# Seven products of quarters in the feed-forward, and attention's value products in one row

## The chip, the cores and the metric

One core of one Trainium2 chip runs the whole program. The metric is the device time of one execution in microseconds. Five engines work beside each other: TensorE (PE, matmul), VectorE (DVE), ScalarE (ACT), GpSimd (POOL) and the queue that starts transfers (SP). Each takes its own instructions in order and waits on the others through semaphores.

## What is computed

One step of a two-layer network for 1024 latent and 256 context tokens of width 1024. Each layer mixes by attention, a recurrence and a long convolution, projects the result out, and ends in a gated feed-forward of inner width 2816:

```python
    mix = jnp.concatenate([att, lru, hy], axis=-1)
    x = x + g1 * (mix @ lp['w_out'])
    h2 = rmsnorm(x, lp['norm2_w']) * (1 + sc2) + sh2
    x = x + g2 * ((jax.nn.silu(h2 @ lp['ffn_w1']) * (h2 @ lp['ffn_w3'])) @ lp['ffn_w2'])
```

## The kernel before, in words

Tokens lie along the free axis and channels along the partitions. The tokens come in three blocks: l0 and l1 (512 latent tokens each) and cc (256 context tokens). All projections are computed at nearly fp32 accuracy: each operand is cut into a high part (rounded to fp32r by ScalarE, L142) and a low part (the difference, on VectorE or GpSimd, L143), and `mm3` (L134) issues three matmuls, high by high, high by low, low by high (L136 to L138). One k-tile of 128 channels by one m-tile of 128 outputs is thus three matmuls of 512 columns for a latent block.

`w_out` (L431) computes the output projection in groups of m-tiles, adds it to the tokens x (L458) and sums squares (`ss_add`, L341). After the last m-tile of a block comes `norm`: TensorE sums the squares over channels (`nps`, L362), VectorE makes the reciprocal root in a dozen tiny steps (L149 to L158), TensorE spreads it (L369), and per k-tile VectorE multiplies (L376), ScalarE adds the shift and rounds (L378) and VectorE or GpSimd makes the low part (L379, L143). These two parts, h, feed the next products.

`ffn` (L470) runs over 22 chunks of 128 inner channels. Per chunk it loads three weight tiles of 512 KB (w1, w3, w2), cut by ScalarE and GpSimd, and per block computes `up` (8 k-tiles of w1 into `pu` and 8 of w3 into `pv`, the context both into `puv`; then the gate on ScalarE and VectorE, L491 to L493, and the cut of g on VectorE) and `down` (8 m-tiles of w2 by g into `py`, each added to x at once, L506). The order of a chunk is up l0, up cc, up l1, down l0, down cc, down l1. In the last chunk the norm of the next layer (or, in the last layer, the store) of each block stands behind its last `down`.

Attention of the latents has 32 units: 4 pairs of heads, 4 runs of 256 queries, layers 0 and 1. A unit does for two heads: scores (`sps`, L685), their evacuation with a running minimum (VectorE, L686), the exponential (ScalarE, L688), transposes of the weights (`tps`, L701) with copies to SBUF by VectorE (L703) or ScalarE (L705), then in `attn_out` the products with the values (`pvo`, L718: 10 tiles of keys by two heads), and four products of 64 rows that spread the reciprocal sums over the head's channels (L722), a product on the result (L727) and its store. A scheduler places all instructions by due times worked out from their order in the program, and pools of buffers with a fixed number each set when a buffer may be written again: weights as loaded (`wst`, 3), weights cut (`whl`, 4).

Of the kernel before, what the change touches and what calls it, by code (L numbers as in the profile page):

```python
# [20 lines left out]
DEPTH = 2  # L21
# [12 lines left out]
FT = 3  # L34
WG = (1, 2)
QT, PQ, PK = 3, 5, 3
# [7 lines left out]
KTB, CMB = 1, 1  # L44
KPIECES = (4, 6, 0, 2)
KORDER = (4, 5, 6, 7, 0, 1, 2, 3)
PE, QX = 4, 2
MORDER = (6, 8, 4, 7, 9, 0, 5, 1, 10, 2, 11, 3, 12, 13, 14, 15)

# [22 lines left out]
class Net:  # L72
# [11 lines left out]
    def setup(self):  # L84
# [13 lines left out]
        for s, n, t in ((self.lat, "l", LAT), (self.ctxs, "c", SEQ)):  # L98
# [12 lines left out]
            s.fe = [self.dp.tile([2, t // 128, 128, 512], F32, name=f"fe_{n}{l}") for l in range(DEPTH)]  # L111
            s.mix = [self.dp.tile([D, t], F32, name=f"mix_{n}{l}") for l in range(DEPTH)]
# [240 lines left out]
    def norm(self, s, l, j, bi, hp, tp):  # L353
# [4 lines left out]
        tag = "s" if l == j == 0 and bi else "n"  # L358
# [9 lines left out]
        for t in range(nt):  # L368
            nc.tensor.matmul(p2[:, t * 128:(t + 1) * 128], r[:, 2 * t:2 * t + 1].to_broadcast([128, 128]),  # L369
                             self.ident, start=True, stop=True)  # L370
        self.h_new(s, bi, hp)
# [59 lines left out]
    def w_out(self, l, hp, tp, xp):  # L431
# [3 lines left out]
        for s, bi, b0, N in blks:  # L435
# [12 lines left out]
            if s.lat:  # L448
                self.x_new(s, bi, xp, 2)
                for d in range(0, 8, XD):  # L450
                    nc.sync.dma_start(s.x[bi][:, d:d + XD], s.xd[bi][:, d:d + XD])

        def one(m, w, s, bi, b0, N):
# [3 lines left out]
            xs = s.x[bi][:, m]  # L457
            nc.vector.scalar_tensor_tensor(xs, ps, self.mod(l, s, 2, m), xs, ALU.mult, ALU.add)  # L458
            self.ss_add(s, tp, s.ss[bi], xs, m)

        for g in GROUPS:
            ws = [self.wtile(self.a["w_out"][l][:, m * 128:(m + 1) * 128].rearrange("(k p) m -> p k m", p=128))
                  for m in g]
            for b in blks:
                for m, w in zip(g, ws):
                    one(m, w, *b)
                if g[-1] == 7:
                    self.norm(b[0], l, 1, b[1], hp, tp)

    def ffn(self, l, hp, pool, last, mods):  # L470
        nc, a = self.nc, self.a
        for c in range(NFF):
            cs = slice(c * 128, (c + 1) * 128)
            w1 = self.wtile(a["ffn_w1"][l][:, cs].rearrange("(k p) m -> p k m", p=128))
            w3 = self.wtile(a["ffn_w3"][l][:, cs].rearrange("(k p) m -> p k m", p=128))
            w2 = self.wtile(a["ffn_w2"][l][cs, :].rearrange("p (k m) -> p k m", m=128))
            gs = {}

            def up(s, bi, b0, N):
                gb = pool.tile([128, 2, N], F32R, tag="g" + s.n, name="g", bufs=3 if s.lat else 1)  # L480
                gs[s, bi] = gb
                if s.lat:
                    pu, pv = self.ps(s, "pu"), self.ps(s, "pv")
                else:
                    pb = self.ps(s, "puv", (128, 2, 256))
                    pu, pv = pb[:, 0], pb[:, 1]
                for w, p in ((w1, pu), (w3, pv)):
                    for k in range(8):
                        self.mm3(p, w[:, 0, k], w[:, 1, k], *self.hk(s, bi, k), k == 0, k == 7)
                t = pool.tile([128, N], F32, tag="ft", name="ft", bufs=FT)  # L490
                nc.scalar.activation(t, pu, AF.Tanh, scale=0.5)  # L491
                nc.vector.scalar_tensor_tensor(t, t, 1.0, pu, ALU.add, ALU.mult)  # L492
                nc.vector.scalar_tensor_tensor(t, t, 0.5, pv, ALU.mult, ALU.mult)  # L493
                self.split(t, gb[:, 0], gb[:, 1], nc.vector)

            def down(s, bi, b0, N):
                gb = gs[s, bi]
                per = 512 // N
                for d0 in range(0, 8, per):
                    ps = self.ps(s, "py", (128, per, N))  # L500
                    for dd in range(per):
# [860 lines left out]
```

## Time and profile before

| | us |
|---|---|
| three runs | 3825.55, 3826.84, 3830.46 (median 3826.84) |
| profiled execution, whole time | 3824.65 |
| its span | 3822.9 |
| busy: TensorE | 3676.4 |
| VectorE | 2148.4 |
| ScalarE | 1155.5 |
| GpSimd | 786.5 |

Busy times overlap; the share of TensorE in the span says that it is nearly always at work. Durations printed for matmuls overlap too, so their pace is read from the distance between starts.

### The profile page before, as it was taken

The numbers are of one execution on the slowest core, as the hardware profiler recorded it, in microseconds if no ns is written. First come the engines' busy times: TensorE is split into PE (matmuls) and PEld (weight loads), VectorE is DVE, ScalarE is ACT, GpSimd is POOL, SyncE is SP. The second block draws the span as 40 slices with busy tenths as digits, with TensorE's granted clock in tenths as the row PEclk, the third lists the DMA queues.
The fourth block names the chain that finished last, engine by engine and source line by source line (L and its number), as shares of the span: only waits on it lengthen the run. The fifth ranks groups of instructions, "written<-read, shape, count | busy, mean of one in ns | idle before, by whom it ended". The sixth has DMA issues, their size and how long they took to land. (4 is left out here: it accounts for less than half of the span.)

```text
span 3822.9 us, 50093 instructions
## 1 busy us (share of the span) xinstructions
PE 3676.4 (96%) x19866; PEld 2936.9 (77%) x19866; DVE 2148.4 (56%) x4242; ACT 1155.5 (30%) x1903; POOL 786.5 (21%) x488
## 2 busy tenths in 40 slices
PE   6999988999999999999998999999999999999999
PEld 3667766676788888888886787666688888888887
DVE  6554567786364544454455674776636444544554
ACT  4333433654231111111124543455423111111111
POOL 3332133100231111211123332200133112111110
PEclk7999999999999999999998999999999999999999
DMA  7554764211211111111113344520311111111111
GB/s 267 176 196 163 231 222 147 69 48 57 87 34 36 43 39 34 39 39 39 34 57 95 110 160 151 181 71 26 108 45 39 39 34 41 38 39 34 45 34 55
DMA packets 292016, 324.90 MB, mean 85 GB/s; under 512 B 26286, under 2 KB 213728, under 8 KB 288454
## 3 DMA queue, kind: packets, MB, share of 16 engines
q1 hardware_dynamic: 288646, 307.02, 24.7%
q0 software_dynamic: 3136, 14.68, 1.2%
q8 instruction: 156, 2.56, 0.3%
q14 instruction: 78, 0.64, 0.1%
HBM read 244.51 MB, written 77.14 MB: 84 GB/s over the span
## 5 line engine op out<-in xcount | busy, mean ns | idle before, releaser
L143 POOL TENSOR_TENSOR whl<-wst,whl 128x1024 fp32r<-128x1024 f32 x177 | 428.6, 2423 | 1976.8 <-ACT whl L142 1921.2
L506 DVE SCALAR_TENSOR_TENSOR x_l<-py,modc,x_l 128x512 f32<-128x512 f32 x704 | 486.2, 738 | 5.1 <-PE py L138 4.8
L142 ACT ACTIVATE whl<-wst 128x1024 fp32r<-128x1024 f32 x180 | 190.1, 1057 | 805.8 <-issue 710.5
L137 PE MATMUL py<-g,whl 128*128 128x512 f32 (+1 forms) x1056 | 376.3, 356 | 0.0
L136 PE MATMUL py<-g,whl 128*128 128x512 f32 (+1 forms) x1056 | 371.4, 358 | 1.5 <-ACT g L142 1.5
L138 PE MATMUL py<-g,whl 128*128 128x512 f32 (+1 forms) x1056 | 369.3, 356 | 0.0
L136 PE MATMUL wps<-h,whl 128*128 128x512 f32 (+1 forms) x768 | 285.0, 373 | 5.6 <-ACT h L378 2.8
L137 PE MATMUL wps<-h,whl 128*128 128x512 f32 (+1 forms) x768 | 283.6, 370 | 2.8 <-POOL h L143 2.0
L492 DVE SCALAR_TENSOR_TENSOR ft<-ft,pu 128x512 f32<-128x512 f32 x88 | 60.6, 689 | 399.7 <-ACT ft L491 399.4
L138 PE MATMUL wps<-h,whl 128*128 128x512 f32 (+1 forms) x768 | 282.9, 369 | 0.0
L136 PE MATMUL pu<-h,whl 128*128 128x512 f32 x704 | 278.5, 396 | 3.2 <-ACT h L378 3.2
L137 PE MATMUL pu<-h,whl 128*128 128x512 f32 x704 | 278.1, 395 | 1.6 <-DVE h L379 1.0
L138 PE MATMUL pv<-h,whl 128*128 128x512 f32 x704 | 278.3, 395 | 0.0
L137 PE MATMUL pv<-h,whl 128*128 128x512 f32 x704 | 277.7, 395 | 0.0
L136 PE MATMUL pv<-h,whl 128*128 128x512 f32 x704 | 277.7, 394 | 0.0
L138 PE MATMUL pu<-h,whl 128*128 128x512 f32 x704 | 277.5, 394 | 0.0
L493 DVE SCALAR_TENSOR_TENSOR ft<-ft,pv 128x512 f32<-128x512 f32 x88 | 60.5, 687 | 345.0 <-PE pv L138 344.7
L138 PEld LDWEIGHTS py<-g,whl 128*128 128x128 f32 x1056 | 198.9, 188 | 32.7
L136 PEld LDWEIGHTS py<-g,whl 128*128 128x128 f32 x1056 | 198.7, 189 | 30.2 <-ACT g L142 1.9
L688 ACT ACTIVATE pq<-pq,mn 128x1280 f32<-128x1280 f32 (+1 forms) x160 | 190.3, 1190 | 104.5 <-DVE pq L686 100.1
L137 PEld LDWEIGHTS py<-g,whl 128*128 128x128 f32 x1056 | 199.6, 189 | 27.0
L701 PE MATMUL tps<-ident,pq 128*128 128x128 f32 x1344 | 202.3, 278 | 14.3 <-ACT pk L705 8.0
(310 smaller groups left out, 7961.6 us busy)
## 6 DMA issues: line engine op xcount, KB each, us to landing
wst<-in_ffn_w_dram SPq DMA_DIRECT2D x132, 512.0 KB
wst<-in_w_mod_dram SPq DMA_DIRECT2D x68, 512.0 KB
wst<-in_w_in_dram SPq DMA_DIRECT2D x32, 512.0 KB
wst<-in_w_mod_dram SPq DMA_DIRECT2D x14, 1024.0 KB
pT_l<-pe SPq DMA_DIRECT2D x40, 256.0 KB
fe_l<-e SPq DMA_DIRECT2D x16, 512.0 KB
qd_l<-qx SPq DMA_DIRECT2D x32, 256.0 KB
eos<-fe_l SPq DMA_DIRECT2D x32, 256.0 KB
```

The lines of the kernel that those rows point to most:

```text
L136: mm(ps, wh, xh, start=first, stop=False)
L137: mm(ps, wh, xl, start=False, stop=False)
L138: mm(ps, wl, xh, start=False, stop=last)
L142: nc.scalar.activation(hi, src, AF.Copy)
L143: (eng or nc.vector).tensor_tensor(lo, src, hi.bitcast(F32), ALU.subtract)
L492: nc.vector.scalar_tensor_tensor(t, t, 1.0, pu, ALU.add, ALU.mult)
L493: nc.vector.scalar_tensor_tensor(t, t, 0.5, pv, ALU.mult, ALU.mult)
L506: nc.vector.scalar_tensor_tensor(xs, ps[:, dd], self.mod(l, s, 5, d), xs, ALU.mult, ALU.add)
L688: nc.scalar.activation(pt, pt, AF.Exp, bias=mn[:, len(chunks) - 1:], scale=-1.0, accum_out=ls[:, t:t + 1])
L701: nc.tensor.transpose(ps[:, k, t], pq[t][:, (t0 + k) * 128:(t0 + k + 1) * 128], self.ident)
```

## The change

The latent tokens and the weights of the feed-forward are taken as 2 x 2 quarters, and each of the three products is computed with seven products of sums and differences of quarters in place of eight products of plain quarters (Strassen's scheme in Winograd's form). For that the feed-forward becomes two stages.

*Output projection and quarters.* `w_out` keeps x of a latent block in two half tiles and also stores it to DRAM (16 stores of 256 KB per layer). `norm_q` normalises in place; `quarters` forms the combinations h11, h21, h22, t1, t2, t3, t4 and cuts each into a high and a low part: 16 sums and differences on VectorE, 28 high parts on ScalarE, 16 low parts on GpSimd, 12 on VectorE.

*`ffn_up`.* 11 steps (`p`), each with two parts (w1, then w3). A part loads two weight tiles, cuts four (w0, w1 as loaded; wb, wa of sums made by VectorE, L624 to L630), issues seven products of 12 matmuls into `pu`, and the context's 48 as before; VectorE combines the seven products to four quarters and gates them. Behind each step five sums on GpSimd make the operands of the next stage, and seven stores of 256 KB bring them to DRAM (`gd`).

*`ffn_down`.* Seven stages (`DOWN`), one for each combined product, each of 11 steps. A step loads one or two quarters of w2 (256 KB each) and one stored operand, adds the quarters where there are two, cuts both operands, and accumulates 12 matmuls into four PSUM banks (`wide`); a stage ends by adding the banks into the one to three quarters of x that take this product. Stages 1 and 3 also compute the context's whole product with w2, with tokens on the partitions, 12 matmuls of 512 columns per half, turned back by transposes (`pyt`). Norms of the next layer stand behind stage 3 (context), 5 (l0) and 6 (l1).

*Attention.* The units are issued in another order (scores two units ahead, queries loaded by unit, six buffers `pq`), the key tiles of the value product run in reverse, and the reciprocal sums are first widened by a GpSimd copy (`rw`), so that two products of 128 rows do the spreading of four of 64.

The core of the diff:

```diff
+            if s.lat:
+                nc.sync.dma_start(s.xd[bi][:, m], xs)
...
+        for d in QORDER:
+            xs = self.xs(s, bi, d)
+            A, B = self.nA[l][1][:, s.cond, d:d + 1], self.mod(l, s, 3, d)
+            nc.vector.scalar_tensor_tensor(xs, xs, A, p2, ALU.mult, ALU.mult)
+            nc.scalar.activation(xs, xs, AF.Identity, bias=B)
...
+        h11, h21 = pair(hb, "hl00"), pair(ha, "hl01")
+        for k in range(4):
+            cut(b11, h11, k, G)
+            cut(b21, h21, k, V)
...
+        for k in range(4):
+            V.tensor_tensor(b11[:, k], b12[:, k], b11[:, k], ALU.subtract)
+            V.tensor_tensor(b12[:, k], b22[:, k], b12[:, k], ALU.subtract)
+            cut(b11, t1, k, G)
+        t3 = (a, low("xq00"))
+        for k in range(4):
+            cut(b12, t3, k, V if k % 2 else G)
+        for k in range(4):
+            cut(b22, h22, k, G)
+            V.tensor_tensor(b22[:, k], b22[:, k], b11[:, k], ALU.subtract)
+            V.tensor_tensor(b21[:, k], b22[:, k], b21[:, k], ALU.subtract)
+        t2 = (b, low("xq10"))
+        for k in range(4):
+            cut(b22, t2, k, V)
+        t4 = (c, low("xq11"))
+        for k in range(4):
+            cut(b21, t4, k, V if k % 2 else G)
...
+        def prod(w, x, b):
+            ps = self.ps(lat, "pu")
+            for k in range(4):
+                self.mm3(ps, w[:, 0, 4 * x + k], w[:, 1, 4 * x + k], b[0][:, k], b[1][:, k], k == 0, k == 3)
...
+                w0 = cut(raw[0])
+                ps = prod(w0, 0, h11)
+                nc.scalar.activation(u, ps, AF.Copy)
+                ps = prod(w0, 1, h21)
+                V.tensor_tensor(c11, ps, u, ALU.add)
+                gate((0, 0), c11, 2)
+                ctx(0, w0)
+                w1 = cut(raw[1])
+                ctx(1, w1)
+                V.tensor_tensor(A22, A21, A22, ALU.add)
+                V.tensor_tensor(A21, A11, A21, ALU.subtract)
+                wb = cut(raw[1])
+                p7 = prod(wb, 0, t3)
+                p5 = prod(wb, 1, t1)
+                V.tensor_tensor(A11, A22, A11, ALU.subtract)
+                V.tensor_tensor(A12, A12, A11, ALU.subtract)
+                wa = cut(raw[0])
+                p6 = prod(wa, 0, t2)
+                V.tensor_tensor(u, p6, u, ALU.add)
+                V.tensor_tensor(c21, p7, u, ALU.add)
+                V.tensor_tensor(u, p5, u, ALU.add)
+                V.tensor_tensor(c22, p5, c21, ALU.add)
+                gate((1, 1), c22, 3)
+                p4 = prod(w1, 1, t4)
+                V.tensor_tensor(c21, c21, p4, ALU.subtract)
+                gate((1, 0), c21, 2)
+                p3 = prod(wa, 1, h22)
+                V.tensor_tensor(c12, p3, u, ALU.add)
+                gate((0, 1), c12, 3)
...
+        for n, (quads, op, q, outs, ctx, nxt) in enumerate(DOWN):
+            wide = [self.ps(lat, "py") for _ in range(4)]
+            for p in range(H):
+                for i in range(len(src)):
+                    nc.sync.dma_start(st[:, i], src[i])
+                nc.sync.dma_start(br, lat.gd[q, p])
+                if ctx:
+                    for j in range(2):
+                        self.split(st[:, j], C[:, j, 0], C[:, j, 1], nc.gpsimd)
+                if len(src) == 2:
+                    nc.vector.tensor_tensor(st[:, 0], st[:, 0], st[:, 1], op)
+                self.split(st[:, 0], A[:, 0], A[:, 1], nc.gpsimd)
+                self.split(br, B[:, 0], B[:, 1], nc.vector)
+                for m in range(4):
+                    c = slice(m * 128, (m + 1) * 128)
+                    self.mm3(wide[m], A[:, 0, c], A[:, 1, c], B[:, 0], B[:, 1], p == 0, p == H - 1)
...
+        rw = pool.tile([128, 2, 2, 64], F32, tag="rw", name="rw", bufs=1)
+        nc.gpsimd.tensor_copy(rw.rearrange("p t h c -> p h t c"), rl.unsqueeze(3).to_broadcast([128, 2, 2, 64]))
-        for t in range(nkt):
+        for t in range(nkt - 1, -1, -1):
```

How it moves instructions is seen at three places. First TensorE in one unit of layer 0's attention, before (`sps` scores, `tps` transposes, `pvo` value products and the spreading):

```order
L718 MATMUL pvo<-pk,vx1l 64x256 x4
L685 MATMUL sps<-kt1l,qx 128x512 x2
L701 MATMUL tps<-ident,pq 128x128 x4
L718 MATMUL pvo<-pk,vx1l 64x256 x4
L685 MATMUL sps<-kt1l,qx 128x512 x2
L685 MATMUL sps<-kt1l,qx 128x256 x2
L718 MATMUL pvo<-pk,vx1l 64x256 x4
L701 MATMUL tps<-ident,pq 128x128 x4
L685 MATMUL sps<-kt1l,qx 128x512 x2
L718 MATMUL pvo<-pk,vx1l 64x256 x3
L722 MATMUL pvo<-ident,rl 64x128 x4
```

and the same place after:

```order
L938 MATMUL pvo<-pk,vx1l 64x256
L903 MATMUL sps<-kt1l,qx 128x512 x2
L903 MATMUL sps<-kt1l,qx 128x256 x2
L919 MATMUL tps<-ident,pq 128x128 x8
L903 MATMUL sps<-kt1l,qx 128x512 x4
L919 MATMUL tps<-ident,pq 128x128 x4
L903 MATMUL sps<-kt1l,qx 128x256 x2
L938 MATMUL pvo<-pk,vx1l 64x256 x19
L941 MATMUL pvo<-ident,rw 128x128 x2
```

The value products stood in runs of three and four among scores and transposes; one now goes first and 19 follow in one row, with two spreading products behind them instead of four.

Second GpSimd, where layer 0's output projection hands over to its feed-forward, before (`whl` weight cuts, `h` low parts of a latent block, `ss` sums of squares):

```order
L143 TENSOR_TENSOR whl<-wst,whl 128x1024 x2
L143 TENSOR_TENSOR h<-nt,h 128x512
L341 TENSOR_TENSOR ss<-ss,sq 128x512
L143 TENSOR_TENSOR h<-nt,h 128x512 x7
L143 TENSOR_TENSOR whl<-wst,whl 128x1024 x63
```

and after (`hq` and `hl` are low parts of quarters, `gs` a sum of gates):

```order
L524 TENSOR_TENSOR hq<-xq_8660,hq 128x512 x4
L160 TENSOR_TENSOR whl<-wst,whl 128x1024
L524 TENSOR_TENSOR hq<-xq_8683,hq 128x512 x3
L524 TENSOR_TENSOR hq<-xq_8660,hq 128x512 x2
L524 TENSOR_TENSOR hq<-xq_8683,hq 128x512
L524 TENSOR_TENSOR hq<-xq_8660,hq 128x512 x2
L524 TENSOR_TENSOR hl<-xq_8682,hq 128x512 x2
L160 TENSOR_TENSOR whl<-wst,whl 128x1024
L524 TENSOR_TENSOR hl<-xq_8661,hq_9624 128x512 x2
L160 TENSOR_TENSOR whl<-wst,whl 128x1024 x4
```

Between the cuts of the first weights there stood eight low parts of the norm; now sixteen cuts of quarters stand there, with two weight cuts among them, and the feed-forward's own cuts come behind.

Third VectorE in a chunk of layer 0's feed-forward, before (`ft` and `g` the gate, `x_l` and `x_c` the results):

```order
L492 SCALAR_TENSOR_TENSOR ft<-ft,pu 128x512
L493 SCALAR_TENSOR_TENSOR ft<-ft,pv 128x512
L506 SCALAR_TENSOR_TENSOR x_l<-py,modc_110,x_l 128x512 x2
L143 TENSOR_TENSOR g<-ft,g 128x512
L506 SCALAR_TENSOR_TENSOR x_l<-py,modc_110,x_l 128x512 x2
L506 SCALAR_TENSOR_TENSOR x_c<-py,modc_110,x_c 128x256 x2
L506 SCALAR_TENSOR_TENSOR x_l<-py,modc_110,x_l 128x512 x3
L506 SCALAR_TENSOR_TENSOR x_c<-py,modc_110,x_c 128x256 x2
```

and in one part of `ffn_up` after (`e` and `g` quarters of the result and its gate, `wst` sums of weights):

```order
L633 TENSOR_TENSOR e<-pu,e 128x512
L635 TENSOR_TENSOR g<-pu,e 128x512
L624 TENSOR_TENSOR wst<-wst 128x512
L636 TENSOR_TENSOR e<-pu,e 128x512
L637 TENSOR_TENSOR g<-pu,g 128x512
L625 TENSOR_TENSOR wst<-wst 128x512
L640 TENSOR_TENSOR g<-g,pu 128x512
L629 TENSOR_TENSOR wst<-wst 128x512
L608 SCALAR_TENSOR_TENSOR g<-e,g 128x512
L630 TENSOR_TENSOR wst<-wst 128x512
L644 TENSOR_TENSOR g<-pu,e 128x512
```

Where additions to x followed each other behind each product of w2, evacuations of the seven products now alternate with the four sums of weights, the first of which (L624) stands ahead of the evacuations L636 and L637.

## Rows read from the trace of the kernel before

**Rows 1.** The page, part 1: busy time, share of the span, instructions
```profile
PE 3676.4 (96%) x19866; PEld 2936.9 (77%) x19866; DVE 2148.4 (56%) x4242; ACT 1155.5 (30%) x1903; POOL 786.5 (21%) x488
```

**Rows 2.** Windows: length, busy time (instructions) by engine, clock, DMA share, GB/s
```profile
510.00:520.00 10.00, 6.43 (x39) 5.91 (x38) 5.20 (x8) 3.73 (x4) 4.97 (x4) 0.76 1.05 407
860.00:960.00 100.00, 99.49 (x686) 68.18 (x682) 64.34 (x181) 46.96 (x74) 0.00 (x0) 1.00 0.15 56
1300.00:1350.00 50.00, 50.00 (x252) 42.17 (x251) 21.63 (x35) 7.39 (x11) 9.61 (x4) 1.00 0.15 43
2010.00:2020.00 10.00, 0.53 (x5) 0.34 (x4) 9.93 (x15) 4.25 (x7) 4.80 (x3) 0.66 0.18 52
2020.00:2030.00 10.00, 5.69 (x15) 4.45 (x16) 9.61 (x21) 8.16 (x17) 3.70 (x4) 0.50 0.01 2
2850.00:2900.00 50.00, 47.61 (x253) 39.99 (x253) 33.84 (x62) 22.38 (x38) 22.82 (x16) 1.00 0.11 32
```

**Rows 3.** Timeline of TensorE, layer 0's feed-forward: start, duration, operation
```profile
1119.02 0.39 PE L136 MATMUL py<-g,whl 128*128 128x512 f32 x1
...
1122.51 0.28 PE L136 MATMUL py<-g,whl 128*128 128x256 f32 x1
...
1123.92 0.39 PE L136 MATMUL py<-g,whl 128*128 128x512 f32 x1
```

**Rows 4.** Groups of one shape (mean ns of one), and one line's durations
```profile
L136 PE MATMUL pu<-h,whl 128*128 128x512 f32 x704 | 278.5, 396 | 3.2 <-ACT h L378 3.2
...
L136 PE MATMUL py<-g,whl 128*128 128x256 f32 x352 | 98.5, 282 | 0.0
...
L722 PE MATMUL pvo<-ident,rl x320: 272/273/322, 664.5 to 2747.4; 128*64 128x128 f32 x160
```

**Rows 5.** Timeline of TensorE in layer 0's attention
```profile
864.69 0.81 PE L722 MATMUL pvo<-ident,rl 128*64 128x128 f32 x6
865.43 0.66 PE L701 MATMUL tps<-ident,pq 128*128 128x128 f32 x4
...
872.80 1.08 PE L718 MATMUL pvo<-pk,vx1l 128*64 128x256 f32 x8
873.82 0.51 PE L685 MATMUL sps<-kt1l,qx 128*128 128x256 f32 x2
...
891.70 1.95 PE L718 MATMUL pvo<-pk,vx1l 128*64 128x256 f32 x16
893.58 1.20 PE L685 MATMUL sps<-kt1l,qx 128*128 128x512 f32 x4
```

**Rows 6.** Timeline of a gate; durations (minimum/median/maximum) of four operations
```profile
1200.56 1.45 DVE L506 SCALAR_TENSOR_TENSOR x_l<-py,modc,x_l 128x512 f32<-128x512 f32 x2
...
1201.05 2.40 POOL L143 TENSOR_TENSOR whl<-wst,whl 128x1024 fp32r<-128x1024 f32 x1 [2.69 <-ACT whl L142]
...
1201.92 2.08 DVE L143 TENSOR_TENSOR g<-ft,g 128x512 fp32r<-128x512 f32 x1
...
L143 DVE TENSOR_TENSOR eo<-eos,eo x32: 665/685/693, 386.4 to 482.8; 128x512 fp32r<-128x512 f32 x32
...
L341 POOL TENSOR_TENSOR ss<-ss,sq x30: 1250/1294/1972, 21.0 to 2879.1; 128x512 f32<-128x512 f32 x30
...
L378 ACT ACTIVATE h<-nt,modc x48: 492/722/726, 67.7 to 2901.6; 128x512 fp32r<-128x512 f32 x32, 128x256 fp32r<-128x256 f32 x16
...
L142 ACT ACTIVATE h<-nt x48: 399/616/635, 69.9 to 2903.4; 128x512 fp32r<-128x512 f32 x32, 128x256 fp32r<-128x256 f32 x16
```

**Rows 7.** DMA issues: a load of 512 KB, us to landing
```profile
fc<-in_c_fcl_dram POOLq DMA_DIRECT2D x12, 512.0 KB, 5.6
```

**Rows 8.** Timeline of TensorE, end of layer 0's feed-forward
```profile
2023.19 1.22 PE L369 MATMUL nps<-ident,nrr 128*128 128x128 f32 x4 [12.66 <-DVE nrr L158]
...
2028.78 0.63 PE L137 MATMUL py<-g,whl 128*128 128x512 f32 x1
...
2029.63 0.63 PE L137 MATMUL py<-g,whl 128*128 128x512 f32 x1
```

More of the change, by code (lines that the diff above doesn't have):

```diff
@@ L370, in norm @@
                              self.ident, start=True, stop=True)
+        return p2
+    def norm(self, s, l, j, bi, hp, tp):
+        nc = self.nc
+        N = s.N
+        p2 = self.norm_r(s, bi, tp, "s" if l == j == 0 and bi else "n")
         self.h_new(s, bi, hp)
@@ L467, in w_out @@
                 if g[-1] == 7:
-                    self.norm(b[0], l, 1, b[1], hp, tp)
-    def ffn(self, l, hp, pool, last, mods):
-        nc, a = self.nc, self.a
[L472 to L483, printed above, removed]
-                else:
[L485 to L501, printed above, removed]
-                        self.mm3(ps[:, dd], w2[:, 0, d0 + dd], w2[:, 1, d0 + dd], gb[:, 0], gb[:, 1], True, True)
-                    for dd in range(per):
-                        d = d0 + dd
-                        xs = s.x[bi][:, d]
-                        nc.vector.scalar_tensor_tensor(xs, ps[:, dd], self.mod(l, s, 5, d), xs, ALU.mult, ALU.add)
-                        if not last and c == NFF - 1:
-                            self.ss_add(s, pool, s.ss[bi], xs, d)
-            l0, l1, cc = self.all
-            if c < NFF - 1:
-                order = ((up, l0), (up, cc), (up, l1), (down, l0), (down, cc), (down, l1))
-            else:
-                def nx(s, bi, b0, N):
-                    if last:
-                        self.store_y(s, bi, pool)
-                        return
-                    self.norm(s, l + 1, 0, bi, hp, pool)
-                    if s.lat:
-                        nc.sync.dma_start(s.xd[bi], s.x[bi])
-                order = ((up, l0), (up, cc), (down, l0), (nx, l0), (down, cc), (up, l1), (nx, cc), (down, l1), (nx, l1))
-            for f, b in order:
-                f(*b)
-            if c < len(mods):
-                self.mods(*mods[c], self.rows, self.ps_l)
@@ new lines, in quarters, with pair, low, cut @@
+    def quarters(self, cp, cq, hp):
+        nc = self.nc
+        ha, hb, _ = hp
+        b11, b21 = self.lat.x[0]
+        b12, b22 = self.lat.x[1]
+        V, G = nc.vector, nc.gpsimd
+        def pair(p, tag):
+            t = p.tile([128, 2, 4, 512], F32R, tag=tag, name="hq")
+            return t[:, 0], t[:, 1]
+        def low(tag):
+            return cp.tile([128, 4, 512], F32R, tag=tag, name="hl")
+        def cut(x, hl, k, eng):
+            nc.scalar.activation(hl[0][:, k], x[:, k], AF.Copy)
+            eng.tensor_tensor(hl[1][:, k], x[:, k], hl[0][:, k].bitcast(F32), ALU.subtract)
+        h11, h21 = pair(hb, "hl00"), pair(ha, "hl01")
+        for k in range(4):
+            cut(b11, h11, k, G)
+            cut(b21, h21, k, V)
+        t1, h22 = pair(hb, "hl10"), pair(hb, "hl11")
+        a, b = pair(cq, "hq1")
+        c = cq.tile([128, 4, 512], F32R, tag="hq4", name="hq4")
+        for k in range(4):
[15 more added lines that the diff above has]
+            cut(b21, t4, k, V if k % 2 else G)
+        return h11, h21, h22, t4, t1, t2, t3
```

229 lines of the change are left out of this document (192 added, 37 removed).

## The prediction, made before the changed kernel was run

> **What bounds the kernel now.** First the page's busy line: TensorE works 96% of the span [rows 1], so what this kernel costs is mostly how many matmuls are issued, and at what pace. Then the windows, for how full TensorE is in each stage: 50.00 of 50 us in the middle of the feed-forward at granted clock 1.00, 99.49 of 100 in attention, 47.61 of 50 where the output projection hands over to the feed-forward, and an empty stretch at the end of layer 0's feed-forward (0.53 of 10 us) [rows 2]. VectorE and GpSimd have slack everywhere in the feed-forward (21.63 and 9.61 us of 50), so today no other engine sets its time. The timeline then prices a matmul by the distance between starts and not by its printed length, since matmuls overlap: 15 products of 512 columns go by from 1119.02 to 1122.51, 0.2327 us each; 12 of 256 columns from 1122.51 to 1123.92, 0.1175 each [rows 3].
>
> The sum is made on the profiled execution, 3824.65 us, and then shifted by 2.19 us to the median of the three runs, 3826.84.
>
> **What goes from TensorE.** *Latent products.* Before, each of the three matrices takes 4224 = 6 x 704 and 2112 = 3 x 704 matmuls of 512 columns ([rows 4] has one of these nine groups of 704). Seven products for eight takes away an eighth: 528 + 264 = 792. Times 0.2327: **-184 us**. *Context's second matrix*: 1056 matmuls of 256 columns (3 x 352, [rows 4]) become 528 of 512, 124.1 against 122.9, less 1; 32 transposes of 128 x 128 turn its result back, at the 0.12 of the broadcasts below, plus 4: **+3**. *Attention.* The broadcasts of L722 halve, 320 to 160 [rows 4], and six take 0.74 us [rows 5]: -20. The value products of a unit stood in five or six pieces among other matmuls and now in two (each product stands as two records in the trace); 8 records take 1.02 us and 16 take 1.88 [rows 5], so one is 0.1075 and each piece costs 0.16 beside its records. I take 0.2, since the switch is paid on the work behind it too: 3.5 pieces x 32 latent units x 0.2 = -22. Against this, one piece of 19 products needs every weight of the second head first, and VectorE, 64.34 of 100 us busy there [rows 2], makes half of these copies and all of the score evacuations; queued behind the unit's first tiles, its last copies end later than its average says. I charge 12 us of new waits (0.4 per unit): **-30**, between -40 and -15. TensorE in all: -184 + 3 - 30 = **-211**.
>
> **What comes on the other engines.** *The quarters, at each layer's start of the feed-forward.* Where normalised tokens went straight into products, 16 sums and differences and 28 cuts into high and low parts now stand ahead. The row that decides is on the port: VectorE's cut of g, whose inputs both lie in SBUF, lasts 2.08 us beside a GpSimd split that runs from 1201.05 to 3.45, and begins to move only when that ends; alone, the same shape takes 0.685, while the accumulations at 1200.56, one input in PSUM, keep their 0.73 beside GpSimd [rows 6]. So these operations of VectorE and GpSimd follow one another. Per layer: 8 VectorE norm steps of l1 (5.9), 24 of VectorE's 28 operations x 0.685 = 16.4, 12 of GpSimd's 16 cuts x 1.294 [rows 6] = 15.5 (the first four of each, for h11 and h21, go with l0's norm), one weight split of 2.40: 40. TensorE has cover until the product that takes the last quarter (p4): 60 latent matmuls (14.0) and 48 of the context (5.6) = 19.6. Leaves 21. Ahead of it ScalarE makes l0's biases and cuts, 8 x (0.722 + 0.616) [rows 6] = 10.7, of which some 6 lie under the projection's last columns: 5. And p2's bank is emptied behind the weight sums in VectorE's queue: 3. So 29 per layer, where the trace of before idles 2.39 [rows 2]: 2 x 26.6 = **+53**. Below, were both engines free of each other, VectorE alone would be 22 against 19.6 of cover, with the 5: 2 x 5 = +10.
>
> The Trainium skill ("SBUF — State Buffer", "SBUF: two separate sides") says of this that a VectorE operation with two SBUF inputs and a GpSimd operation that reads SBUF lock each other out for a whole instruction. The row of 2.08 agrees, and so does the accumulation that is not held up; by the rule this term is 53, without it 10.
>
> *Up, steady state, 2 x 11 x 2 = 44 parts.* A part is 84 latent matmuls (19.5) and 48 of the context (5.6): 25.2 us of TensorE. GpSimd has four splits (9.6) and some 3 us of the gate's sums, VectorE eight to ten operations with both inputs in SBUF (5.6), so the shared port is busy 18 of 25: enough on the average. The order on VectorE is the risk: the sums of weights for the last split stand between the evacuations of PSUM, and the evacuation that frees p5's bank stands behind L624, which waits for GpSimd's second split. Following the queue, the bank comes free 8.8 us into the cycle where TensorE wants it at 8.4: 0.4 x 44 = **+18**. The bounds are 0 and one more GpSimd split and its low cut on the chain (3.1 us a part): 136.
>
> *Down, seven stages of 11 steps.* A step is 12 latent matmuls, 2.79 us, in the two context stages 24, 5.58. Per step the shared port takes, in those two stages, 3 GpSimd cuts and 3 VectorE operations, 3 x (1.294 + 0.685) = 5.94: over by 0.36, and with the sums of squares at their ends 6 us for each of 4 such stages: 24. In stages 4 to 6 it takes 1.294 + 2 x 0.685 = 2.66, just under, but each step brings 768 KB, which at 2.79 us is 282 GB/s, of the 407 that a window of this trace reached [rows 2], through three buffers whose cycle of load, sum, cut and cut is 5.6 us for a load of 512 KB [rows 7] + 0.685 + 0.6 + 1.294 = 8.2, against 3 x 2.79 = 8.4: no room for anything in the queues. I charge a quarter of a microsecond a step, 3 us in each of 6 stages: 18. Twelve times a stage begins behind the emptying of four banks, 1 us: 12. Together **+54**; with nearly everything hidden 15, at the upper end twice as much, 110 (1 us on each of the 66 steps of stages 4 to 6 and on the 44 of the context). *Hand-over* from up to down, a store and a load of 256 KB deep: **+4**.
>
> *End of layer 0's feed-forward.* The 12.66 us in which TensorE waits for l1's norm, and the restart at granted clock 0.50, the level of 1.2 GHz, where matmuls stand 0.425 apart (2028.78 to 2029.63) [rows 8], are partly covered: l0's and the context's norms now lie under later stages. I take back **-11** (0 to -14).
>
> **Sum.** 53 + 18 + 54 + 4 - 11 = +118; -211 + 118 = -93; 3824.65 - 93 + 2.19 = 3733.8, so **3734 us**.
>
> **Rivals.** *A. The port costs little*: quarters +10, up 0, down 15, the rest as above: +18; 3827 - 211 + 18 = **3634**. For it: steady-state averages all lie under TensorE's time. Against it: the 2.08 us row. *B. Down starves*: three buffers do not hide load and cut, down is 110: **3790**. For it: one operand now comes back from DRAM and 768 KB per 2.79 us has no counterpart in the feed-forward of before, which moves 43 GB/s [rows 2]. *C. Slower*: up's chain is a split longer than I followed it, so that every part waits 3.1 us: 3734 + 118 = **3852**. It decides from 2.5 us a part on (0.4 + 93 / 44). Against it: the tile order lets a split begin as soon as a buffer is free, and four buffers stand in the cycle. *D. Slower by the clock*: down's 110 steps without context products are bursts of 12 matmuls with a wait behind each; granted clock fell to 0.50 behind the 12.66 us wait [rows 8], yet stayed 1.00 around the 2.39 us of idling [rows 2]. Were it to fall at each short wait, 1320 matmuls at 0.425 in place of 0.2327: +254, **3988**; it decides from 480 such matmuls on. The Trainium skill ("TensorE: Matmul & The Clock Gate", "HAM oscillation — how this bites in real kernels") tells of a kernel whose short bursts between DMA waits restarted at the low clock each time; the rows here show it for a long wait only. *E. Attention does not gather*: with VectorE late for the one piece, only the broadcasts' 20 us less the waits remain; 20 us more than forecast, inside the main case.
>
> **Chances.** Forecast 0.57, A 0.20, B 0.15, C 0.05, D 0.03. The range 3624 to 3804 takes in the forecast with its bounds, A and B, and leaves out C and D and tails. A measurement of this kernel tells 0.2% (8 us) from no change. Faster by more: 0.89; within: 0.04 (the tail of B); slower: 0.07.
>
> **What would show it.** Right: in the up stage TensorE full but for a fraction of a microsecond per part, waiting for a VectorE evacuation; a gap or two of 10 to 20 us in all at each layer's first part, put down to cuts of the quarters, with VectorE cuts of about 2 us beside GpSimd's; down stages 4 to 6 and the context's with waits under a microsecond put down to the loaded quarters or the cuts; value products in rows of 38 trace records and VectorE over 70% in attention; granted clock 1.00 in all of these. Wrong: if the quarters' gap is under 5 us, exclusion was overcharged; if up waits over 2 us per part on GpSimd's splits, C; if down idles a third of its time behind DMA, B; if its clock reads below 1.00, D.

## The result, and the profile after

The changed kernel takes 3720.98 us (median of four runs, 3711.6 to 3722.05) where the kernel before takes 3826.2 beside it: ratio 0.972, 95% interval 0.9705 to 0.9735, faster by 105 us. Forecast were 3734 us, 93 faster than the median shown, within 3624 to 3804. The profiled execution, from which all rows of after are read, is the one of 3711.6 us; its span of 3709.8 is 113 shorter than before's 3822.9.

The page's busy line, to be held against [rows 1]: TensorE has 179 us less work and GpSimd 653 more.

```profile
PE 3497.4 (94%) x18418; PEld 2785.8 (75%) x18418; DVE 2331.7 (63%) x4016; ACT 1433.2 (39%) x2347; POOL 1439.6 (39%) x940
```

The windows of after, to be held against [rows 2] (columns as there): the start of layer 0's feed-forward, its up stage, the last products of its down stage 3 with most of stage 4, the passage to stage 5, and the end of layer 1's feed-forward.

```profile
1100.00:1122.00 22.00, 13.96 (x37) 9.68 (x37) 19.43 (x22) 8.52 (x13) 12.52 (x8) 0.59 0.02 7
1172.00:1656.40 484.40, 484.40 (x2528) 412.29 (x2528) 292.26 (x334) 119.99 (x158) 247.47 (x123) 1.00 0.26 85
1844.00:1876.00 32.00, 31.97 (x137) 26.17 (x138) 23.70 (x37) 15.45 (x28) 15.50 (x12) 0.95 0.77 246
1876.00:1913.00 37.00, 33.69 (x149) 27.42 (x148) 33.61 (x52) 16.46 (x32) 18.30 (x15) 0.95 0.70 228
3660.00:3700.00 40.00, 33.21 (x142) 27.42 (x143) 17.45 (x21) 11.58 (x20) 9.48 (x7) 0.91 0.52 170
```

The second row is the whole middle of the up stage: 484.40 of 484.40 us. Most of a down stage is full too (31.97 of 32). What the change gives back lies between: the quarters at the start (13.96 of 22 us, granted clock 0.59), the passages from one down stage to the next (33.69 of 37), and layer 1's last stage, where TensorE has 33.21 of 40.

By stages, each from the end of TensorE's last product of one to that of the next:

| stretch | before | after | difference |
|---|---|---|---|
| start to layer 0's output projection | 1081.8 | 1072.0 | -9.8 |
| from there to layer 1's input projection | 1238.3 | 1179.0 | -59.3 |
| layer 1's mixing, to its output projection | 553.7 | 542.4 | -11.3 |
| layer 1's feed-forward and the stores | 949.0 | 916.4 | -32.6 |

Of after, the second stretch is up 584.4, down 301.9 and input projection 292.8; the last is up 585.7 and down with the stores 330.8.

### The profile page after: what moved, and what is told of

Its sections match the earlier page's. It is cut to its first block, busy times and chain, and to the rows that moved or that the text cites. A ratio compares the mean times of both kernels' runs of the same rounds, so it can differ in the third digit from the quotient of the medians.

```text
span 3709.8 us, 50289 instructions
## 1 busy us (share of the span) xinstructions
PE 3497.4 (94%) x18418; PEld 2785.8 (75%) x18418; DVE 2331.7 (63%) x4016; ACT 1433.2 (39%) x2347; POOL 1439.6 (39%) x940
## 4 chain that ended last, share of the span: by engine, by line
PE 60%; DVE 7%; DMA 7%; issue 4%; POOL 2%; ACT 2%; SPq 0%; DVEq 0%; ACTq 0%; POOLq 0%
PE pu L154 8%; PE pu L155 8%; PE pu L153 8%; PE pvo L938 4%; PE sps L903 4%; PE tps L919 3%; PE puv L153 2%; PE puv L154 2%; PE puv L155 2%; PE ops L155 2%; PE ops L154 2%; PE ops L153 2%; DMA wst<-in_ffn_w_dram 2%; POOL whl L160 2%; PE py L153 2%
## 5 line engine op out<-in xcount | busy, mean ns | idle before, releaser
L160 POOL TENSOR_TENSOR whl<-wst,whl 128x512 fp32r<-128x512 f32 (+1 forms) x463 | 894.0, 1940 | 864.0 <-ACT whl L159 842.7
L159 ACT ACTIVATE whl<-wst 128x512 fp32r<-128x512 f32 (+1 forms) x488 | 394.3, 825 | 853.5 <-PE pu L155 297.9
L153 PE MATMUL pu<-hq,whl 128*128 128x512 f32 x1232 | 490.0, 399 | 10.2 <-ACT hq L523 8.8
L155 PE MATMUL pu<-hq,whl 128*128 128x512 f32 x1232 | 488.9, 398 | 0.0
L154 PE MATMUL pu<-hq,whl 128*128 128x512 f32 x704 | 281.4, 400 | 8.7 <-POOL hq L524 4.6
L153 PEld LDWEIGHTS pu<-hq,whl 128*128 128x128 f32 x1232 | 234.2, 190 | 65.5 <-ACT hq L523 10.7
L155 PEld LDWEIGHTS pu<-hq,whl 128*128 128x128 f32 x1232 | 234.6, 190 | 55.1
L153 PE MATMUL py<-whl 128*128 128x512 f32 x616 | 224.2, 402 | 23.4 <-ACT whl L159 18.0
L154 PE MATMUL py<-whl 128*128 128x512 f32 x616 | 228.9, 396 | 0.2 <-DVE whl L160 0.2
L155 PE MATMUL py<-whl 128*128 128x512 f32 x616 | 221.0, 395 | 0.7 <-POOL whl L160 0.6
L154 PE MATMUL pu<-hl,whl 128*128 128x512 f32 x528 | 210.6, 399 | 8.8 <-POOL hl L524 8.8
L155 PE MATMUL puv<-h,whl 128*128 128x256 f32 x704 | 199.2, 283 | 5.2 <-POOL whl L160 5.2
L153 PE MATMUL puv<-h,whl 128*128 128x256 f32 x704 | 199.6, 283 | 0.3 <-ACT whl L159 0.3
L154 PE MATMUL puv<-h,whl 128*128 128x256 f32 x704 | 199.2, 283 | 0.0
L701 DVE TENSOR_TENSOR wst<-wst 128x512 f32<-128x512 f32 x110 | 133.8, 1219 | 102.3 <-POOL whl L160 68.9
L919 PEld LDWEIGHTS tps<-ident,pq 128*128 128x128 f32 x1344 | 156.4, 142 | 53.6 <-DVE pk L921 21.8
L904 DVE TENSOR_SCALAR_CACHE_REDUCE pq<-sps,mn 128x512 f32<-128x512 f32 (+1 forms) x256 | 155.8, 611 | 50.3 <-PE sps L903 46.0
```

The lines of the kernel that those rows point to most:

```text
L153: mm(ps, wh, xh, start=first, stop=False)
L154: mm(ps, wh, xl, start=False, stop=False)
L155: mm(ps, wl, xh, start=False, stop=last)
L159: nc.scalar.activation(hi, src, AF.Copy)
L160: (eng or nc.vector).tensor_tensor(lo, src, hi.bitcast(F32), ALU.subtract)
L701: nc.vector.tensor_tensor(st[:, 0], st[:, 0], st[:, 1], op)
```

## The experiments

Each was timed in three rounds against the kernel before, on the same chip. The changed kernel itself, run again so:

> The changed kernel itself, for the chip that the other three run on: ratio 0.972 to the kernel before (0.9705 to 0.9735).

It gave 3715.65 against 3821.41, ratio 0.9719 (0.9704 to 0.9733). Times of the others are therefore compared by ratio, and where a few microseconds matter by the stages of their traces, which in the two traces of the changed kernel repeat within 1 us in the up stages (584.4 and 584.6, 585.7 and 586.0), within 2 in the down stages (301.9 and 303.9, 330.8 both times) and within 4 in the mixing stages.

**The quarters' cuts on VectorE.** In `quarters`, after l1's norm:

```diff
-            cut(b11, t1, k, G)
+            cut(b11, t1, k, V)
...
-            cut(b12, t3, k, V if k % 2 else G)
+            cut(b12, t3, k, V)
...
-            cut(b22, h22, k, G)
+            cut(b22, h22, k, V)
...
-            cut(b21, t4, k, V if k % 2 else G)
+            cut(b21, t4, k, V)
```

> The changed kernel with the twelve GpSimd cuts that follow l1's norm in quarters done by VectorE instead. Changed kernel: 3721 median, its profile 3711.6. Theory 1 (VectorE operations with two SBUF inputs and GpSimd operations follow one another): the chain of 24 x 0.60 + 12 x 1.29 + 2.4 becomes 36 x 0.60 + 2.4, 8 us shorter per layer, so 10 to 16 us faster than the changed kernel; the differences that now last 1.76 us last 0.6 to 0.7. Theory 2 (the engines run freely beside each other and VectorE's own queue sets the end): VectorE gets 12 x 0.60 = 7 us more per layer, so 10 to 15 us slower.

Ratio 0.9689 (0.9674 to 0.9704), 3702.47 us: some 11 us faster than the changed kernel, though VectorE has twelve operations more per layer. The timelines of GpSimd and VectorE in the changed kernel (start, duration, operation):

```profile
1096.66 10.20 POOL L524 TENSOR_TENSOR hq<-xq,hq 128x512 fp32r<-128x512 f32 x6 [1.08 <-ACT hq L523]
...
1097.25 1.76 DVE L535 TENSOR_TENSOR xq<-xq,xq 128x512 f32<-128x512 f32 x1
1098.93 1.75 DVE L534 TENSOR_TENSOR xq<-xq,xq 128x512 f32<-128x512 f32 x1
1100.61 3.45 DVE L535 TENSOR_TENSOR xq<-xq,xq 128x512 f32<-128x512 f32 x2
```

Six cuts run on GpSimd without a gap from 1096.66 to 1106.86, and in that time each of VectorE's differences takes 1.75 us. VectorE's same differences with GpSimd out of the way:

```profile
1097.59 0.69 DVE L524 TENSOR_TENSOR hq<-xq,hq 128x512 fp32r<-128x512 f32 x1
1098.19 0.69 DVE L535 TENSOR_TENSOR xq<-xq,xq 128x512 f32<-128x512 f32 x1
1098.80 0.69 DVE L534 TENSOR_TENSOR xq<-xq,xq 128x512 f32<-128x512 f32 x1
```

0.60 from start to start. The up stages go from 584.4 and 585.7 to 579.9 and 581.5. So theory 1 is right in sign, and free engines are excluded; the gain is 9 us in these stages where 10 to 16 were expected. Part of the shortfall is that VectorE and GpSimd are not strictly one after the other: a pair takes 1.70, not 0.60 + 1.29 = 1.89, so that twelve pairs are worth 6 us a layer, and the last low cut does end 47.1 us into layer 0's stage in place of 53.1. Of these 6 us, 4.5 and 4.2 reach the end of the stage; where the rest stays was not followed.

**The store's own ring.** The operands of the down stages (`gr`) and the staging tiles of the final store (`yr`) had one ring of three buffers:

```diff
-            yr = pool.tile([128, D], F32, tag="gl", name="yr", bufs=3)
+            yr = pool.tile([128, D], F32, tag="yr", name="yr", bufs=2)
```

> The changed kernel with the staging tiles of the final store (yr) in two buffers of their own, where they shared a ring of three with the operands that the down stages load. Theory 1: the 5.98 and 7.09 us of waiting in layer 1's last stage are the ring: loads of operands stand behind the store of l0, and the down stage of layer 1 (320 us, 19 more than layer 0's) gets shorter; 8 to 17 us faster than the changed kernel's 3721. Theory 2: the store's own transfers and transposes fill that time, the transfers and the loads share the DMA engines: within 3 us of 3721.

3697.51 us, ratio 0.9674 (0.9659 to 0.9689), some 17 us faster than the changed kernel; the last stretch, down and stores of layer 1, goes from 330.8 to 317.4 us, and the up and down stages ahead of it stay within 1 us. In the changed kernel, TensorE, SP's queue and ScalarE around that place:

```profile
3654.35 5.34 PE L335 MATMUL yps<-ident,x_l 128*128 128x128 f32 x32 [5.98 <-DVE x_l L726]
3666.79 2.07 PE L153 MATMUL py<-whl 128*128 128x512 f32 x4 [7.09 <-ACT whl L159]
...
3635.51 21.03 SPq L689 DMA_DIRECT2D wst<-in_ffn_w_dram  x16
3658.47 3.87 SPq L342 DMA_DIRECT2D out_y_sample_dram<-yr  x4
3662.45 9.43 SPq L695 DMA_DIRECT2D gr<-gd_l  x7
...
3666.11 1.27 ACT L159 ACTIVATE whl<-gr 128x512 fp32r<-128x512 f32 x2 [4.28 <-DMA gr<-gd_l]
```

TensorE waits 5.98 us for the results of stage 5 that the store wants to turn, then 7.09 for the first operand of stage 6. SP has issued all 16 loads of weights ahead (3635.51), but a load of an operand only behind the four stores of `yr` (3658.47, then 3662.45): the ring. With a ring of its own the waits of that stretch are (waited for: us in total, times, longest)

```profile
PE py L153 <- ACT whl L159: 6.4, 6, 3.3
PE yps L335 <- DVE x_l L726: 4.8, 3, 3.8
```

where the first was 12.0, 5, 7.1 in the changed kernel.

**A version faster than both kernels.** The two edits together:

> The changed kernel with both edits that gained by themselves: the quarters' later cuts all on VectorE, and the final store's staging in a ring of its own. The two lie in different stages (start of the feed-forward 9 us over both layers, end of layer 1 13 us), so if each gain stood on the path they add: 22 us faster than the changed kernel, ratio about 0.966. If either only moved its waiting elsewhere: under 15.

3687.08 us (3682.09 to 3694.92), ratio 0.9649 (0.963 to 0.9668): 29 us faster than the changed kernel on the same chip. The gains add.

**Early products in the first step.** On top of that version, w3's first tile with its products and its context product goes ahead of the products that wait for quarters (the parts of a step as functions, the order of the first step changed):

```diff
-            for part, src in enumerate((a["ffn_w1"][l], a["ffn_w3"][l])):
...
+            else:
+                r0, u0 = head(0)
+                w10 = second(0, r0)
+                r1, u1 = head(1)
+                tail(0, r0, u0, w10)
+                tail(1, r1, u1, second(1, r1))
```

> On top of both (ratio 0.9649, 3687 us): in the first step of the up stage, w3's first weight tile, its two products with h11 and h21 and its context product go ahead of the products that wait for the later quarters, so 24 latent and 24 context matmuls (8.4 us at 0.2327 and 0.1175) stand where TensorE waits; VectorE's chain of quarters is unchanged. Theory: what TensorE waits there (up stage 579.9 and 579.2 us where 554 us of products stand in it) is cover that is missing, so both up stages get 5 to 8 us shorter, 10 to 16 together, ratio about 0.961. Rival: the added gates on VectorE and the two more splits on GpSimd lengthen the chain of quarters by as much as the cover grows: within 3 us.

3688.29 us, ratio 0.965 against 0.9649 without: nothing. The up stages take 579.2 and 581.5 us against 579.9 and 579.2. The rival is right: with the quarters' cuts on VectorE it has no time to spare. The window that answers to the first row of the windows above, without the early products and then with them (the third busy time is VectorE's):

```profile
1100.00:1122.00 22.00, 16.30 (x57) 11.90 (x58) 21.90 (x35) 9.85 (x16) 2.64 (x1) 0.72 0.02 7
```

```profile
1100.00:1122.00 22.00, 16.46 (x52) 11.42 (x52) 21.96 (x39) 11.05 (x19) 0.00 (x0) 0.78 0.07 24
```

21.90 and 21.96 of 22 us. The early gates go between the operations that make the quarters, and push these back by at least what they cover: the last low cut ends 58.8 us into layer 0's stage in place of 47.2, and TensorE's waits for low parts are still there.

```profile
PE pu L154 <- DVE hl L524: 5.0, 3, 2.4
```

**Loads of operands left out.** In the four stages without context products the stored operand is loaded in the first step alone; the loads of weights, two thirds of the bytes of a step in stages 4 to 6, all stay.

```diff
-                if n:
+                if n in (2, 4, 5, 6):
+                    if p == 0:
+                        gr = pool.tile([128, 2, 512], F32, tag="gl", name="gr", bufs=3)
+                    br = gr[:, 0]
+                elif n:
...
+                if p == 0 or n not in (2, 4, 5, 6):
+                    nc.sync.dma_start(br, lat.gd[q, p])
```

> The changed kernel, but in the four down stages without context products the stored operand is loaded once per stage (its first step) and used for all 11 steps: 80 loads of 256 KB fewer, the output is not the reference's. All cuts and sums stay. Theory 1 (the shared port and the emptying of banks set what down loses, the loads are hidden): within 4 us of 3721, apart from layer 1's last stage, where loads wait for the ring shared with the store, up to 10 us. Rival (B of the prediction: down waits for its transfers): over 15 us faster.

3711.78 us, ratio 0.9715: no difference to be measured. Layer 0's down stage takes 302.2 us against 301.9; layer 1's end gains 7.7, at the ring. So the loads of the stored operands are not what down waits for, beyond the first step of a stage. The weights' loads are not tested by this kernel, and in the changed kernel the chain that ended last passes through one of them ahead of layer 0's stage 5 and through another ahead of stage 6 (start, duration):

```profile
1883.64 3.65 DMA wst<-in_ffn_w_dram
1918.49 3.63 DMA wst<-in_ffn_w_dram
```

TensorE's waits in layer 0's down stage, in the changed kernel and then here:

```profile
PE py L153 <- ACT whl L159: 6.0, 6, 2.2
PE pyc L155 <- DVE gk L160: 4.7, 3, 2.0
PE py L153 <- DVE x_l L726: 3.3, 1, 3.3
```

```profile
PE pyc L155 <- DVE gk L160: 4.7, 3, 2.0
PE py L154 <- DVE whl L160: 3.8, 3, 2.5
PE py L153 <- ACT whl L159: 3.3, 4, 2.0
```

**Low cuts of down's weights on VectorE**, on top of the two edits that gained:

```diff
-                self.split(st[:, 0], A[:, 0], A[:, 1], nc.gpsimd)
+                self.split(st[:, 0], A[:, 0], A[:, 1], nc.vector if n > 2 else nc.gpsimd)
```

> On top of both: in down stages 3 to 6 the low cut of the weight operand is VectorE's instead of GpSimd's. By the prediction's account of the shared port stage 3 goes from 5.94 to 5.33 us a step, under TensorE's 5.58, and stages 4 to 6 from 2.66 to 2.06: its 0.36 us of excess a step goes, 5 to 8 us over both layers. By the waits in the changed kernel's trace (pyc waits for VectorE's cut gk, 4.7 us a layer, and 5 us for ScalarE's first cuts of a stage) VectorE's queue is what is late there, and more work in it makes the down stages longer, by up to 10 us.

Ratio 0.966 (0.9644 to 0.9677) against 0.9649 without: no difference in the whole time. In the traces the down stages are 2.5 and 2.9 us shorter (302.8 to 300.3; 316.7 to 313.8), together 5.4: the sign of the port's account and the lower end of its 5 to 8. Other stages of the same traces differ by as much, and the whole time is not shorter, so this stays unsettled.

**Four more evacuations in the up stage.**

```diff
-                V.tensor_tensor(c21, p7, u, ALU.add)
+                for _ in range(5):
+                    V.tensor_tensor(c21, p7, u, ALU.add)
```

> The changed kernel with the evacuation of p7 in the up stage (L637) written five times in place of once: four more VectorE operations of 0.60 us, 2.4 us a part, ahead of those that free p5's bank, 44 parts. By the prediction's step (that bank comes free 0.4 us late as it is) this costs 44 x 2.4 = 105 us. By the trace of the changed kernel (TensorE 484.40 of 484.40 us busy, VectorE waits for TensorE ahead of L633 for 5.5 us a part) there is room for it: under 15 us.

The up stages take 584.0 and 585.3 us: the 106 us of additional work cost nothing there. The wait of VectorE for TensorE ahead of L633 from 1172 to 1650, in the second trace of the changed kernel and then in this one, and this kernel's window:

```profile
DVE e L633 <- PE pu L155: 109.4, 19, 7.1
```

```profile
DVE e L633 <- PE pu L155: 83.4, 19, 7.1
...
1172.00:1650.00 478.00, 478.00 (x2503) 407.75 (x2502) 305.23 (x401) 122.08 (x156) 244.57 (x121) 1.00 0.27 85
```

VectorE waits 26 us less there, and TensorE is as full as before. The rest of the 46 us that these 19 parts gain in work comes mostly out of operations with two SBUF inputs that now last shorter beside GpSimd (L608 1.00 us on the mean for 1.59, L629 0.68 for 1.03). The whole is 8 us slower than the changed kernel on the same chip (3723.63, ratio 0.9744), and the down stages are longer by more than that (311.0 for 303.9, and 336.3 for 330.8 at the end). Their code is the same; their instructions were placed in another order. Why that order is worse was not followed.

**Attention.** Three kernels. First attention whole as before:

> The changed kernel with attention as in the kernel before (order of units, value products in pieces, spreading with four products of 64 rows, five buffers of scores). Theory 1 (my sum, mended by the traces: 10 us per layer up to the end of the output projection): 3721 + 21 = 3742. Rival: the gain of attention came from somewhere else in the new placement (the first tiles of the feed-forward): within 5 us of 3721.

3730.44 us, ratio 0.9762 (0.9746 to 0.9779): 16 us of the 21, and 19 in the two mixing stages of its trace. Then the old spreading of the sums:

```diff
-        rw = pool.tile([128, 2, 2, 64], F32, tag="rw", name="rw", bufs=1)
...
-            nc.tensor.matmul(ob[:, 1, t * 128:(t + 1) * 128], rw[:, t].rearrange("p h c -> p (h c)"), self.ident,
...
+            for hd in range(2):
+                nc.tensor.matmul(ob[64 * hd:64 * hd + 64, 1, t * 128:(t + 1) * 128],
+                                 rl[:, hd, t:t + 1].to_broadcast([128, 64]), self.ident, start=True, stop=True)
```

> The changed kernel with the spreading of reciprocal sums by four products of 64 rows as before (the GpSimd copy rw is gone), while the value products stay in rows of 19. By the prediction's terms (-20 for the halved spreading, -22 + 12 for the pieces) it loses 20 of attention's 22 us. Rival (the gain is mostly from the pieces and the order of units, and TensorE would have waited anyhow): it loses under 8.

3710.32 us, ratio 0.9708 (0.9693 to 0.9724): nothing is lost. Last, the key tiles in forward order:

```diff
-        for t in range(nkt - 1, -1, -1):
+        for t in range(nkt):
...
```

> The changed kernel with the key tiles of the value products in forward order: the units, the score buffers and the widened sums stay, the products fall into four to six pieces again. Theory (each switch between pieces costs 0.2 us, and this is attention's gain): the steady unit goes from 15.45 back to 16.3 us, 3716 + 22 = 3738. Rival (the gain is the new order of units, scores issued two units ahead): the unit stays at 15.45 and the time within 5 us of the changed kernel's.

3726.9 us, ratio 0.9751 (0.9736 to 0.9766), 12 us slower than the changed kernel, of the 16 that attention as before loses; in the mixing stages of the traces it is 10 of 19. The value products stand in five pieces again. A steady unit, from one end of the spreading to the next, takes 16.8 and 15.8 us by turns in the kernel before, 15.4 and 15.5 in the changed one, 15.3 to 15.5 with the old spreading, and 16.5, 15.9 and 15.8 in turn with the forward order. So the rows of 19 are between half and three quarters of the gain, the order of units at most the rest, and the spreading gains nothing. The timeline of TensorE in a unit of the changed kernel, and with the old spreading:

```profile
870.48 4.53 PE L938 MATMUL pvo<-pk,vx1l 128*64 128x256 f32 x38
874.94 0.71 PE L941 MATMUL pvo<-ident,rw 128*128 128x128 f32 x4
875.49 1.04 PE L919 MATMUL tps<-ident,pq 128*128 128x128 f32 x8
```

```profile
870.48 4.32 PE L936 MATMUL pvo<-pk,vx1l 128*64 128x256 f32 x37
874.42 0.38 PE L940 MATMUL pvo<-ident,rl 128*64 128x128 f32 x2
...
874.64 0.81 PE L940 MATMUL pvo<-ident,rl 128*64 128x128 f32 x6
875.37 0.51 PE L903 MATMUL sps<-kt1l,qx 128*128 128x256 f32 x2
```

Four records of 128 rows take 0.55 us (874.94 to 875.49), eight of 64 rows 0.95 (874.42 to 875.37). But from the start of the row to the wide products it is 4.46 us (870.48 to 874.94), to the narrow ones 3.94, so what the wide ones save is lost ahead of them: from the start of the row to the product behind the spreading it is 5.01 us with the wide products and 4.89 with the narrow ones. TensorE's time per unit is not shorter, and TensorE is nearly full here, in the changed kernel as with the old spreading:

```profile
830.00:930.00 100.00, 99.06 (x693) 74.94 (x692) 74.51 (x219) 54.36 (x86) 2.82 (x7) 1.00 0.07 22
```

```profile
830.00:930.00 100.00, 99.06 (x722) 76.07 (x720) 74.56 (x218) 52.93 (x84) 0.00 (x0) 1.00 0.07 21
```

## Why the prediction was right, and where it was not

The sum came out 13 us too slow for the median and 20 for the profile. By its terms, from the table of stages (profile to profile):

| term | forecast | measured |
|---|---|---|
| products of the feed-forward | -181 | -185 |
| attention | -30 | -21 |
| quarters | +53 | +52 |
| up, steady | +18 | 0 |
| down and hand-over | +58 | +61, of it 13 the store's ring |
| end of layer 0's feed-forward | -11 | about -20, a remainder |

The layer 1 part of the down row, 33, is likewise what remains of the last stretch.

*Products.* In the middle of up 2528 records take 484.40 us, so a part of 132 takes 25.29 us, 0.1 more than the forecast 25.19, over 44 parts +4 us. In the down stages 24 products go by in 5.44 us (3622.81 to 3628.25 below), 2.72 a step of 12 where 2.79 was taken, and a context step takes 5.57 for 5.58: over 55 steps of the one and 22 of the other, twice, -8. So the pace from [rows 3] held within 3%.

*Quarters.* The up stages are 22 x 25.29 = 556.4 us of products; 584.4 and 585.7 leave 28.0 and 29.3, less the 2.39 of before each: 52.5. (By TensorE's starts the norm's small products are 3.6 us of the 28.0, and 2.8 of before's stretch too; like against like it is about 47.) The mechanism, exclusion as in [rows 6], is shown by the cuts that were taken off GpSimd. The rule of the Trainium skill that the prediction names ("SBUF — State Buffer", "SBUF: two separate sides") holds by these rows, but for the 0.19 us by which a pair is shorter than its two parts. The waits stand where they were expected (layer 0's start):

```profile
PE pu L153 <- ACT hq L523: 5.4, 2, 2.9
PE pu L154 <- POOL hl L524: 4.3, 1, 4.3
PE pu L154 <- POOL hq L524: 2.5, 1, 2.5
PE pu L154 <- DVE hq L524: 2.0, 1, 2.0
```

Not every part of the 29 stands where it was put. The 5 us for ScalarE's cuts of l0 ahead of the first products are not there, since TensorE is full for the first 10 us, and no wait of 3 us for p2's bank is seen; ScalarE's waits of 5.4 belong to later quarters.

```profile
1072.00:1082.00 10.00, 10.00 (x80) 9.70 (x80) 8.71 (x14) 9.52 (x16) 6.42 (x5) 1.00 0.38 116
```

The forecast also left out the clock: it took 1.00 for granted here. From 1100 on, between these waits, TensorE ran at the lower level, 1.2 GHz, 0.43 between starts, and rose again only after the last of them (start, duration; the wait in brackets):

```profile
1113.69 0.79 PE L154 MATMUL pu<-hl,whl 128*128 128x512 f32 x1 [4.31 <-POOL hl L524]
1114.28 0.63 PE L155 MATMUL pu<-hq,whl 128*128 128x512 f32 x1
1114.71 0.63 PE L153 MATMUL pu<-hq,whl 128*128 128x512 f32 x1
...
1118.63 0.40 PE L155 MATMUL pu<-hq,whl 128*128 128x512 f32 x1
```

That the term fits all the same is partly chance: the pure waiting of that part is 18 us in layer 0 (14.2 in the rows of waits above, the others are for weight cuts), and the slow products and the norm's small ones make up most of the rest. How much the clock adds to the stage is not isolated: a slow product between two waits also takes the place of waiting, and the eleven behind the last wait, from 1113.69 to 1118.40, cost some 2 us by estimate (4.7 in place of 11 x 0.2327).

*Up, steady.* The failed step is "the bank comes free 8.8 us into the cycle where TensorE wants it at 8.4". VectorE's L624 doesn't wait for GpSimd's second split, which is done by then, and VectorE waits for TensorE (5.5 us a part); 2.4 us more of work found room. GpSimd's split had been put too late in that queue.

*Attention.* The spreading, -20, is worth nothing: its price was taken from its own records, and what the wide products save there is lost between the row and them. The pieces, -22 + 12, are worth 10 to 12 of the 21, but made up otherwise: in a steady unit three pieces fewer save 0.62 us (15.47 for the mean of 16.5, 15.9 and 15.8), the 0.2 a piece of the forecast, while only some 19 of the 32 units run at the steady pace (19 x 0.62 = 12), and the 12 us charged for waits are not seen in the steady stretch (TensorE 99.06 of 100). Of the 9 to 11 that are left, 2 to 5 stay with attention as before, and for the others the order of units, which was not in the sum, is the candidate, not shown by a run of its own.

*Down.* Layer 0's 301.9 us hold 55 x 2.72 + 22 x 5.57 = 272.1 of products and 2 of transposes: 28 us over, where 29 were forecast, 27 for the stage and 2 for the hand-over. It is made up otherwise. Within a stage nearly every step goes at TensorE's pace, those of stages 4 to 6 too, so the 0.25 and 0.36 us a step that were charged for the port and the buffers are mostly not there; the context stages wait 4.7 us for `gk` in all. Most of what is lost otherwise lies at the beginnings of stages, ScalarE's first cuts (6.0) and the emptying of the banks (3.3), so that a first step takes 5 to 7 us instead of 2.72. These three waits are 14 of the 28 us; how the norms' small products and slow products share the rest was not followed. One such beginning, in layer 1:

```profile
3619.51 0.50 PE L153 MATMUL py<-whl 128*128 128x512 f32 x1 [1.75 <-DVE x_l L726]
...
3622.81 0.39 PE L154 MATMUL py<-whl 128*128 128x512 f32 x1
...
3628.25 0.39 PE L155 MATMUL py<-whl 128*128 128x512 f32 x1
```

The loads of the stored operands are hidden, as the kernel without them shows; of the weights' loads that is not shown, and the two on the chain ahead of stages 5 and 6 speak against it. In layer 1 another 13 us go to the shared ring, which no view of before could show and the diff did: `yr` and `gr` have the same tag.

*End of layer 0.* The stretch of [rows 8] with TensorE empty is gone; a shorter restart at the lower clock stays (granted clock 0.66 from 1980 to 1990). Around this place, before and after:

```profile
1990.00:2060.00 70.00, 52.96 (x273) 44.46 (x273) 53.34 (x101) 33.97 (x60) 31.91 (x25) 0.86 0.23 83
```

```profile
1950.00:2020.00 70.00, 63.70 (x314) 51.35 (x312) 34.32 (x53) 34.65 (x56) 35.53 (x21) 0.95 0.50 153
```

TensorE idles 17.0 us before and 6.3 after: 11 less, the size that was forecast. The -20 of the table is what remains of the second stretch's -59.3 when half the products (-92.6), the quarters (+25.6) and the down stage (+27.8) are taken out; it holds all that is not accounted for there.

*Rivals.* A is out for the quarters (exclusion costs about what the forecast said) and right for up; B, at 110 for down, is out by size (61, or 48 without the ring), and for the stored operands by the kernel without their loads, while the weights' loads were not tested; C is out, as TensorE is full in the middle of up and stays so with more evacuations; D is seen at the quarters, and in the down stages only a little, at their passages (0.91 to 0.95).

## What to carry to other kernels

Before a stage of many small vector operations is added, sort them by whether both inputs lie in SBUF, and put those of one stage on one engine: here GpSimd's help with twelve cuts cost 9 us more than doing them on VectorE. In a steady stage, look which engine waits for which; a chain followed by hand through two queues was late by several microseconds. When a stage begins to load operands, see who else uses the tag of their buffers.

## What the runs showed of the hardware

A VectorE operation with two SBUF inputs takes 0.69 us alone and 1.75 beside a busy GpSimd, and a pair of the two takes 1.70 from start to start, a little less than their sum of 1.89. Products that only spread a column cost 0.1375 us per record with 128 rows and 0.119 with 64; halving their number took 0.4 us off their own 0.95, and nothing off the time from the row of value products ahead of them to the product behind (5.01 us against 4.89). Among the quarters' waits of 2 to 4.3 us the granted clock of a stretch of 22 us was 0.59, while 2.39 us of idling in 50 had left it at 1.00 in the kernel before [rows 2].
